# A bidirectional GLA and RWKV-7 encoder block: one-pass gate product, low-rank operands fetched a unit ahead, two operands made at another place

## The chip, the cores and the metric

The kernel is one program on one core of a Trainium2 chip. The metric is the device time in microseconds (us) of one execution, from start to end. A core has five engines with queues of their own: TensorE (PE), VectorE (DVE), ScalarE (ACT), GpSimd (POOL) and SyncE (SP); in this kernel SP issues all the DMAs.

## The reference

One layer on x of 2048 x 1024, all in float32:

```python
h = rmsnorm(x); p = h @ W_in                   # GLA | RWKV-7 | merge-gate columns
# GLA, 4 heads, forward (f) and backward (b): the decay of each step is a low-rank gate
la_f = log_sigmoid(af @ wa2_f + ba_f) / 16     # af: 16 columns of p; wa2: 16 x 256
la_b = log_sigmoid(ab @ wa2_b + ba_b) / 16
yA = (rmsnorm(gla(q, k, v, la_f) + flip(gla(flip(q, k, v, la_b)))) * silu(og)) @ proj
# RWKV-7, 8 heads, both directions
s = p + mu_prev * (shift_prev(p) - p) + mu_next * (shift_next(p) - p)
r, k, v, wl, al, gl = split(s)
w_dir = exp(-exp(-softplus(-(w0_dir + tanh(wl) @ w2_dir)) - 0.5))
a = sigmoid(a0 + al @ a2); g = sigmoid(gl) @ g2
kk = normalise(k * k_k); k = k * (1 + (a - 1) * k_a)
S = S * w + (S @ -kk)(kk * a)^T + v k^T; y = S r          # scan over 2048 steps
bonus = sum(r * k * r_k) * v
yB = ((groupnorm(y_f + y_b) + bonus) * g) @ proj
x = x + (sigmoid(gA) * yA + sigmoid(gB) * yB) @ W_out
x = rmsnorm(x + conv_glu(rmsnorm(x)))
```

## The kernel before

Products that need full precision are made of two float32r parts each: `split` rounds an operand to a high part and subtracts it for a low part, and `mm3` multiplies high by high, high by low and low by high. A float32 product without such parts is issued as two instructions.

The stages follow each other. First the norm of x and the v columns. Then `waf`, the 32 columns of the gates' low-rank input: for each of the 4 time blocks of 512 steps, 16 matmuls give 64 rows in PSUM (rows 0 to 31 from the weight's high part, 32 to 63 from its low part), which one copy puts into an `ev` buffer (a pool of three) and one store writes to the scratch `d_af` (L393 to L406). `gla_load` (L469) fetches a block of `d_af` for each of 4 heads x 4 blocks; `gla_gate` (L486) multiplies it by `wa2`, in which both row halves hold the same weights, in float32: `z` (L491).

The projections run tile by tile (`in_tile`, L373). Between their time blocks `Weave` steps a side generator: all of GLA first, then the RWKV preparation. The preparation goes over 4 head pairs p and 4 blocks b, which gives 16 units of `rwkv_prep(p, b)` (L725). A unit loads `twal`, the block of tanh(wl) and al (one buffer), and for b = 0 `lora`, the pair's weights; makes the shifted `sk`, `sr`, `sv`; multiplies `lora` by `twal` three times (L741 twice, L747 once, the tile `pw` has two banks); makes the scan's operands `arbk` (three buffers, L782 to L789), stored to `d_lt`; transposes v (L799, stored at L803); and makes the bonus (L805 to L812), for which `sr` is overwritten at L805 and multiplied by a matrix of ones at L807.

The order in each engine's queue, SP's DMA queue included, is chosen when the program is built, by a planning pass that goes by the order in the code and by modelled durations. Only the scan's main loop (L1283 on) keeps a hand-made order. The scan's start loads `Lt` tiles and makes scores (`sc_mm`, `sc_ev`), and between its pieces `fil(n)` takes n steps of the generator `fill` (L1127): the rest of the gate projections, four matmuls of 512 columns to a step (L1218). `w_get` loads a weight into the one `wraw` buffer (L1154), `w_put` splits it into `whi` and `wlo` (two buffers). The first step of the generator only loads the first weight; the second splits it and multiplies.

Of the kernel before, what the change touches and what calls it, by code (L numbers as in the profile page):

```python
# [104 lines left out]
def _pack(inputs):  # L105
# [8 lines left out]
    a["waf"] = kt(w[:, 1536:1568])  # L114
    wa = np.zeros((64, 4, 128), np.float32)
    f, b = one("gla_wa2_f"), one("gla_wa2_b")
    for h in range(4):
        for r0 in (0, 32):
            wa[r0:r0 + 16, h, :64] = f[:, h * 64:h * 64 + 64]
            wa[r0 + 16:r0 + 32, h, 64:] = b[:, h * 64:h * 64 + 64]  # L120
# [46 lines left out]
def _body(tc, A, out, dump=None, upto=99):  # L167
# [11 lines left out]

    def scratch(name, shape):  # L180
        return dr.tile(shape, F32, name=name, tag=name)

    d_gla = scratch("d_gla", [8, 128, T])
    d_vg = scratch("d_vg", [T, 512])
    d_af = scratch("d_af", [64, T])
    d_rw = scratch("d_rw", [14, 128, T])
# [212 lines left out]
    for b in range(NB):  # L399
        ps = pg.tile([128, 512], F32, name="pg", tag="pg")  # L400
        for i, xx in enumerate((hhi, hlo)):
            for k in range(KT):
                nc.tensor.matmul(ps[0:64, :], whi[:, k, 0:64], xx[b][:, k, :], start=(i == 0 and k == 0), stop=(i == 1 and k == KT - 1))
        o = ev.tile([128, 512], F32, name="ev", tag="ev")
        nc.scalar.copy(out=o[0:64, :], in_=ps[0:64, :])
        sync.dma_start(out=d_af[:, b * BT:(b + 1) * BT], in_=o[0:64, :])  # L406

# [15 lines left out]
    nc.vector.tensor_copy(out=gdiag, in_=gdf)  # L423
    wa2 = gp.tile([64, 4, 128], F32, name="wa2")
    sync.dma_start(out=wa2, in_=A["wa2"])
    dec = gp.tile([128, 4, 16], F32, name="dec")
# [42 lines left out]
    def gla_load(hs, b):  # L469
# [4 lines left out]
        ts = slice(b * BT, (b + 1) * BT)  # L474
        af = gp.tile([64, 512], F32, name="af", tag="af", bufs=1)
        sync.dma_start(out=af, in_=d_af[:, ts])
        q2 = gp.tile([128, 512], F32, name="q2", tag="q2", bufs=2)
# [245 lines left out]
    PE_ = {(d, j): nc.vector if (d, j) in DV else nc.gpsimd for d in range(2) for j in range(4)}  # L723

    def rwkv_prep(p, b):  # L725
        ts = slice(b * BT, (b + 1) * BT)
        cs = slice(b * 8, b * 8 + 8)
        pc = slice(p * 128, p * 128 + 128)
        twal = R["rp"].tile([128, 512], F32, name="twal", tag="twal")
        sync.dma_start(out=twal, in_=d_twal[:, ts])  # L730
        sk = shifted(3 + 3 * p, b, "sk")
        sr = shifted(2 + 3 * p, b, "sr")
        sv = shifted(4 + 3 * p, b, "sv")
        if b == 0:
            R["lora"] = R["rp"].tile([128, 2, 128], F32, name="lora", tag="lora")
            sync.dma_start(out=R["lora"], in_=A["lora"][:, :, pc])
        sg = []
# [15 lines left out]
        act_tail[0] = last  # L753
        yield

        tmp = R["rp"].tile([128, 512], F32, name="tmp", tag="tmp")
# [37 lines left out]
        yield  # L794
        nc.scalar.copy(out=tmp, in_=sv[:, ::-1])
        for d, sx in enumerate((sv, tmp)):
            pv = R["rs"].tile([128, 4, 128], F32, name="pv", tag="pv")
# [6 lines left out]
        yield  # L804
        nc.vector.scalar_tensor_tensor(out=sr, in0=sr, scalar=vc("rk", p), in1=kp, op0=ALU.mult, op1=ALU.mult)  # L805
        pn = R["rs"].tile([128, 512], F32, name="pn", tag="pn", bufs=2)
# [320 lines left out]
    def fill():  # L1127
# [39 lines left out]
        for i, u in enumerate(fresh):  # L1167
            if i:
                at(puts[i - 1], w_get, u)
            at(puts[i], w_put, u)  # L1170

# [31 lines left out]

        w_get(0)
        yield
        for i, (u, h, ph) in enumerate(order_):
# [26 lines left out]
    def fil(n=1):  # L1233
        for _ in range(n):
            next(fl, None)

    load_x(0)
    for e in range(2):
# [596 lines left out]
```

## Time and profile before

| | |
|---|---|
| three runs | 3526.49, 3528.93 (median), 3532.44 us |
| profiled execution: own time | 3531.8 us |
| its span, first to last instruction | 3530.0 us |
| mean granted clock of TensorE | 0.961 |
| instructions | 58016 |

The rows of the profile that are quoted below come from this one execution. Times in them are us from the start of the span unless marked ns. A line number is a line of the kernel before. The granted clock is a share of full speed; it has two levels, 1.2 and 2.4 GHz. Names of tiles stand without their numbers, so `wa` is `wa2`, and `whi` any of its buffers; `out<-in` is what an instruction writes and reads. A matmul's record includes its latency, so records in a row overlap; the distance from start to start is what one takes of the engine.

### The profile page before, as it was taken

Reading aid. Unit: us, or ns where it says so; the run is one execution under the profiler, and the core shown is the slowest. Engines: PE = TensorE matmul, PEld = TensorE weight load, DVE = VectorE, ACT = ScalarE, POOL = GpSimd, SP = SyncE. Lnnn points to the kernel's source line nnn. Section 1 sums busy time; section 2 is a strip of 40 time slices with the busy share of each in tenths; the row PEclk is TensorE's granted clock in tenths of the full one; section 3 lists DMA queues with packets and bytes.
Section 4 is the critical chain, followed back from the end, with each engine's and each line's share of the span. In section 5 each row is a group of like instructions: output and inputs, shape, how many; then the busy total and the mean of one; then the engine's idle time right before and its main releaser. Section 6 shows DMA issues by size and latency. Waiting matters only on the chain.

```text
span 3530.0 us, 58016 instructions
## 1 busy us (share of the span) xinstructions
PE 3282.4 (93%) x22232; PEld 2626.9 (74%) x22232; DVE 2281.4 (65%) x3903; ACT 1609.0 (46%) x2912; POOL 875.7 (25%) x715
## 2 busy tenths in 40 slices
PE   7999999999988888887777999999999999999999
PEld 6787778766656777766666788888877888878887
DVE  5207664587865666666776566888989989623222
ACT  4214443455545776776644333544454444411111
POOL 1122222134440000000002411666665555000000
PEclk9999999999999998998888999999999999999999
DMA  4233343687875455556788846422242222523222
GB/s 150 94 117 108 127 141 122 187 227 224 232 214 180 150 183 157 171 184 195 229 254 282 294 142 191 134 81 89 79 136 96 84 84 78 182 82 112 80 85 63
DMA packets 403222, 531.29 MB, mean 151 GB/s; under 512 B 61504, under 2 KB 250560, under 8 KB 402944
## 3 DMA queue, kind: packets, MB, share of 16 engines
q1 hardware_dynamic: 402944, 527.58, 48.0%
q8 instruction: 175, 2.87, 0.3%
q14 instruction: 103, 0.84, 0.1%
HBM read 345.02 MB, written 181.93 MB: 149 GB/s over the span
## 4 chain that ended last, share of the span: by engine, by line
PE 48%; DVE 12%; DMA 6%; ACT 4%; issue 2%; SPq 1%; POOL 0%; DVEq 0%; ACTq 0%; POOLq 0%
PE pu L1638 20%; PE pg L241 6%; PE pd L1722 4%; PE pd L1724 4%; PE pd L1723 4%; PE pf L1218 3%; DVE tm L924 1%; DVE XX L925 1%; DMA d_m<-ev 1%; DMA wraw<-win 1%; DVE X L1027 1%; DVE gX L1004 1%; DVE wlo L227 1%; ACT TT L938 1%; DMA ev<-d_gate 1%
## 5 line engine op out<-in xcount | busy, mean ns | idle before, releaser
L227 POOL TENSOR_TENSOR wlo<-wraw,whi 128x1024 fp32r<-128x1024 f32 x46 | 115.3, 2507 | 1175.0 <-ACT whi L226 929.1
L1561 POOL TENSOR_TENSOR rw<-rw 128x512 f32<-128x512 f32 x168 | 282.1, 1694 | 72.4 <-DVE s3l L227 59.7
L1722 PE MATMUL pd<-wdh,whi 128*128 128x512 f32 x672 | 261.6, 391 | 0.9 <-DVE ug L1506 0.9
L1723 PE MATMUL pd<-wdl,whi 128*128 128x512 f32 x672 | 261.4, 389 | 0.0
L1724 PE MATMUL pd<-wdh,wlo 128*128 128x512 f32 x672 | 259.3, 389 | 0.0
L1218 PE MATMUL pf<-fop,whi 128*128 128x512 f32 x576 | 178.6, 448 | 85.3 <-ACT whi L226 58.3
L241 PE MATMUL pg<-hlo,whi 128*128 128x512 f32 x928 | 254.2, 407 | 0.0
L241 PE MATMUL pg<-hhi,whi 128*128 128x512 f32 x928 | 249.7, 404 | 3.1 <-ACT whi L226 3.1
L241 PE MATMUL pg<-hhi,wlo 128*128 128x512 f32 x928 | 248.2, 402 | 0.0
L241 PEld LDWEIGHTS pg<-hhi,whi 128*128 128x128 f32 x928 | 176.2, 192 | 55.9 <-issue 15.8
L241 PEld LDWEIGHTS pg<-hlo,whi 128*128 128x128 f32 x928 | 176.9, 194 | 53.9 <-issue 18.1
L241 PEld LDWEIGHTS pg<-hhi,wlo 128*128 128x128 f32 x928 | 176.1, 192 | 50.6 <-issue 14.3
L1218 PEld LDWEIGHTS pf<-fop,whi 128*128 128x128 f32 x576 | 114.1, 209 | 122.1 <-ACT whi L226 64.1
L226 ACT CAST whi<-wraw 128x1024 fp32r<-128x1024 f32 x114 | 119.5, 1048 | 112.9 <-PE pg L241 54.1
L1606 DVE SCALAR_TENSOR_TENSOR cv<-ug,vec,cv 128x511 f32<-128x511 f32 (+1 forms) x88 | 124.1, 1410 | 57.4 <-ACT cv L1605 57.4
L1711 ACT CAST whi<-wraw 128x1024 fp32r<-128x1024 f32 (+1 forms) x36 | 35.3, 980 | 267.1 <-PE pd L1723 186.6
L1722 PEld LDWEIGHTS pd<-wdh,whi 128*128 128x128 f32 x672 | 126.1, 188 | 29.9 <-issue 4.2
L1724 PEld LDWEIGHTS pd<-wdh,wlo 128*128 128x128 f32 x672 | 126.1, 188 | 26.2
L1723 PEld LDWEIGHTS pd<-wdl,whi 128*128 128x128 f32 x672 | 126.1, 188 | 25.7
L1613 ACT ACTIVATE cv<-cv 128x511 f32<-128x511 f32 (+1 forms) x84 | 53.3, 634 | 197.0 <-DVE cv L1607 197.0
L1714 DVE TENSOR_TENSOR wlo<-wraw,whi 128x1024 fp32r<-128x1024 f32 (+1 forms) x36 | 39.3, 1091 | 151.4 <-ACT whi L1711 151.4
L227 DVE TENSOR_TENSOR wlo<-wraw,whi 128x1024 fp32r<-128x1024 f32 x68 | 84.1, 1237 | 79.3 <-ACT whi L226 79.2
(482 smaller groups left out, 8119.9 us busy)
## 6 DMA issues: line engine op xcount, KB each, us to landing
rw<-wup SPq DMA_DIRECT2D x84, 512.0 KB, 3.5
wraw<-win SPq DMA_DIRECT2D x74, 512.0 KB, 4.3
Lt<-d_lt SPq DMA_DIRECT2D x64, 512.0 KB, 5.2
d_lt<-arbk SPq DMA_DIRECT2D x96, 256.0 KB, 3.9
d_gate<-ev SPq DMA_DIRECT2D x64, 256.0 KB, 3.7
X<-d_vt SPq DMA_DIRECT2D x64, 256.0 KB, 4.4
bj<-d_lt SPq DMA_DIRECT2D x128, 128.0 KB, 3.8
d_m<-ev SPq DMA_DIRECT2D x64, 256.0 KB, 5.3
```

Of the source, the lines that this page charges most:

```text
L226: (hi_eng or nc.scalar.copy)(out=hi, in_=src)
L227: (lo_eng or nc.vector).tensor_tensor(out=lo, in0=src, in1=hi.bitcast(F32), op=ALU.subtract)
L241: nc.tensor.matmul(ps, (wh, wh, wl)[ph], (xh, xl, xh)[ph], start=(ph == 0 and i == 0), stop=(ph == 2 and i == n - 1))
L1218: nc.tensor.matmul(ps, (wh, wh, wl)[ph][:, k0 + k, :], (hi, lo, hi)[ph][:, k, :], start=i == first[u] and k == 0, stop=i == last[u] and k ...
L1561: ps_ = lambda o, x, y, op: nc.gpsimd.tensor_tensor(out=o, in0=x, in1=y, op=op)
L1606: nc.vector.scalar_tensor_tensor(out=c, in0=u[:, c0 - 1:c0 - 1 + n], scalar=vc("cw0", m), in1=c, op0=ALU.mult, op1=ALU.add)
L1613: nc.scalar.activation(out=g, in_=g, func=AF.Silu)
L1638: nc.tensor.matmul(ps, w_, x_, start=first and n == 0, stop=n == len(mm) - 1, skip_group_check=True)
L1714: nc.vector.tensor_tensor(out=al[:, 0:m], in0=raw[:, 0:m], in1=ah[:, 0:m].bitcast(F32), op=ALU.subtract)
L1722: nc.tensor.matmul(ps, a, wdh[k][:, cs], start=(k == 0), stop=False)
L1723: nc.tensor.matmul(ps, a, wdl[k][:, cs], start=False, stop=False)
L1724: nc.tensor.matmul(ps, l, wdh[k][:, cs], start=False, stop=False)
```

## The change

It has four parts. The gates' operand gets 128 rows: the high part of the first 32 rows of PSUM, its low part, the rows of the weight's low part, and the high part once more, against `wa2` in high part (96 rows) and low part (32 rows); the product is then one float32r instruction of 128 rows. For this each block makes a second `ev` tile with a subtraction and four stores rather than one. `twal` and `lora` are loaded by `get_low`, for the next unit, behind the present unit's third product in the code. The overwriting of `sr` stands ahead of the transposes of v. And `fil(1)` takes the first step of `fill` ahead of the scan's loads, with the first split in it; the later steps come one call sooner.

```diff
--- before.py
+++ after.py
@@ -112,10 +112,10 @@
     a["win"] = np.stack([kt(w[:, c]).reshape(128, 1024) for c in _in_tiles()])
     a["wv"] = kt(w[:, 512:1024])
     a["waf"] = kt(w[:, 1536:1568])
-    wa = np.zeros((64, 4, 128), np.float32)
+    wa = np.zeros((128, 4, 128), np.float32)
     f, b = one("gla_wa2_f"), one("gla_wa2_b")
     for h in range(4):
-        for r0 in (0, 32):
+        for r0 in (0, 32, 64, 96):
             wa[r0:r0 + 16, h, :64] = f[:, h * 64:h * 64 + 64]
             wa[r0 + 16:r0 + 32, h, 64:] = b[:, h * 64:h * 64 + 64]
     a["wa2"] = wa
@@ -177,12 +177,12 @@
 
     dr = pool(base, "dr", space=DRAM)
 
-    def scratch(name, shape):
-        return dr.tile(shape, F32, name=name, tag=name)
+    def scratch(name, shape, dt=F32):
+        return dr.tile(shape, dt, name=name, tag=name)
 
     d_gla = scratch("d_gla", [8, 128, T])
     d_vg = scratch("d_vg", [T, 512])
-    d_af = scratch("d_af", [64, T])
+    d_af = scratch("d_af", [128, T])
     d_rw = scratch("d_rw", [14, 128, T])
     d_gate = scratch("d_gate", [16, 128, T])
     d_oa = scratch("d_oa", [4, 128, T])
@@ -401,9 +401,13 @@
         for i, xx in enumerate((hhi, hlo)):
             for k in range(KT):
                 nc.tensor.matmul(ps[0:64, :], whi[:, k, 0:64], xx[b][:, k, :], start=(i == 0 and k == 0), stop=(i == 1 and k == KT - 1))
-        o = ev.tile([128, 512], F32, name="ev", tag="ev")
+
+        o = ev.tile([128, 512], F32R, name="ev", tag="ev")
+        ol = ev.tile([128, 512], F32R, name="ev", tag="ev")
         nc.scalar.copy(out=o[0:64, :], in_=ps[0:64, :])
-        sync.dma_start(out=d_af[:, b * BT:(b + 1) * BT], in_=o[0:64, :])
+        nc.vector.tensor_tensor(out=ol[0:32, :], in0=ps[0:32, :], in1=o[0:32, :].bitcast(F32), op=ALU.subtract)
+        for r0, src in ((0, o[0:32]), (32, ol[0:32]), (64, o[32:64]), (96, o[0:32])):
+            sync.dma_start(out=d_af[r0:r0 + 32, b * BT:(b + 1) * BT], in_=src.bitcast(F32))
 
 
     s1 = ExitStack()
@@ -421,8 +425,11 @@
     gdf = ev.tile([128, 512], F32, name="ev", tag="ev")[:, 0:128]
     sync.dma_start(out=gdf, in_=A["c_gdiag"])
     nc.vector.tensor_copy(out=gdiag, in_=gdf)
-    wa2 = gp.tile([64, 4, 128], F32, name="wa2")
-    sync.dma_start(out=wa2, in_=A["wa2"])
+    wa2 = gp.tile([128, 4, 128], F32R, name="wa2")
+    war = ev.tile([128, 4, 128], F32, name="ev", tag="ev")
+    sync.dma_start(out=war, in_=A["wa2"])
+    nc.scalar.copy(out=wa2, in_=war)
+    nc.vector.tensor_tensor(out=wa2[96:128], in0=war[96:128], in1=wa2[96:128].bitcast(F32), op=ALU.subtract)
     dec = gp.tile([128, 4, 16], F32, name="dec")
     b4 = [128, 4, 128]
     v4 = lambda t: t.rearrange("p (a b) -> p a b", a=4)
@@ -472,8 +479,8 @@
         qsrc = d_gla[(h // 2) * 2, r0:r0 + 64, :]
         ksrc = d_gla[(h // 2) * 2 + 1, r0:r0 + 64, :]
         ts = slice(b * BT, (b + 1) * BT)
-        af = gp.tile([64, 512], F32, name="af", tag="af", bufs=1)
-        sync.dma_start(out=af, in_=d_af[:, ts])
+        af = gp.tile([128, 512], F32R, name="af", tag="af", bufs=1)
+        sync.dma_start(out=af.bitcast(F32), in_=d_af[:, ts])
         q2 = gp.tile([128, 512], F32, name="q2", tag="q2", bufs=2)
         k2 = gp.tile([128, 512], F32, name="k2", tag="k2", bufs=2)
         for r in (0, 64):
@@ -722,18 +729,23 @@
 
     PE_ = {(d, j): nc.vector if (d, j) in DV else nc.gpsimd for d in range(2) for j in range(4)}
 
+    def get_low(p, b):
+        R["twal"] = R["rp"].tile([128, 512], F32, name="twal", tag="twal")
+        sync.dma_start(out=R["twal"], in_=d_twal[:, b * BT:(b + 1) * BT])
+        if b == 0:
+            R["lora"] = R["rp"].tile([128, 2, 128], F32, name="lora", tag="lora")
+            sync.dma_start(out=R["lora"], in_=A["lora"][:, :, p * 128:p * 128 + 128])
+
     def rwkv_prep(p, b):
         ts = slice(b * BT, (b + 1) * BT)
         cs = slice(b * 8, b * 8 + 8)
         pc = slice(p * 128, p * 128 + 128)
-        twal = R["rp"].tile([128, 512], F32, name="twal", tag="twal")
-        sync.dma_start(out=twal, in_=d_twal[:, ts])
+        if (p, b) == (0, 0):
+            get_low(0, 0)
+        twal = R["twal"]
         sk = shifted(3 + 3 * p, b, "sk")
         sr = shifted(2 + 3 * p, b, "sr")
         sv = shifted(4 + 3 * p, b, "sv")
-        if b == 0:
-            R["lora"] = R["rp"].tile([128, 2, 128], F32, name="lora", tag="lora")
-            sync.dma_start(out=R["lora"], in_=A["lora"][:, :, pc])
         sg = []
         last = act_tail[0]
         for d in range(2):
@@ -752,6 +764,8 @@
             last = nc.scalar.preload_act_table_set(LNEXP)
         act_tail[0] = last
         yield
+        if (p, b) != (3, NB - 1):
+            get_low(p + (b + 1) // NB, (b + 1) % NB)
 
         tmp = R["rp"].tile([128, 512], F32, name="tmp", tag="tmp")
         kk = R["rp"].tile([128, 512], F32, name="kkt", tag="kkt")
@@ -793,6 +807,7 @@
         act_tail[0] = fin
         yield
         nc.scalar.copy(out=tmp, in_=sv[:, ::-1])
+        nc.vector.scalar_tensor_tensor(out=sr, in0=sr, scalar=vc("rk", p), in1=kp, op0=ALU.mult, op1=ALU.mult)
         for d, sx in enumerate((sv, tmp)):
             pv = R["rs"].tile([128, 4, 128], F32, name="pv", tag="pv")
             for c in range(4):
@@ -802,7 +817,6 @@
             vs = slice((NB - 1 - b) * BT, (NB - b) * BT) if d else ts
             sync.dma_start(out=d_vt[vs, d, pc].rearrange("(c q) e -> q c e", q=128), in_=o.rearrange("p (a b) -> p a b", a=4))
         yield
-        nc.vector.scalar_tensor_tensor(out=sr, in0=sr, scalar=vc("rk", p), in1=kp, op0=ALU.mult, op1=ALU.mult)
         pn = R["rs"].tile([128, 512], F32, name="pn", tag="pn", bufs=2)
         nc.tensor.matmul(pn, bones, sr, start=True, stop=True)
         o = R["rp"].tile([128, 512], F32, name="pev", tag="pev", bufs=2)
@@ -1167,7 +1181,7 @@
         for i, u in enumerate(fresh):
             if i:
                 at(puts[i - 1], w_get, u)
-            at(puts[i], w_put, u)
+                at(puts[i], w_put, u)
 
         def o_new(k, b, h):
             ops[k, b, h] = [hb.tile([128, 4, BT], F32R, name="fop", **FOP) for _ in range(2)]
@@ -1202,6 +1216,7 @@
                 at(last[u], g_sig, u)
 
         w_get(0)
+        w_put(0)
         yield
         for i, (u, h, ph) in enumerate(order_):
             for f, a_ in sorted(todo.get(i, []), key=lambda x: x[0] not in (o_put, w_put)):
@@ -1234,6 +1249,7 @@
         for _ in range(n):
             next(fl, None)
 
+    fil(1)
     load_x(0)
     for e in range(2):
         for d in range(2):
```

## Rows read from the trace of the kernel before

**Rows 1.** The page, busy us, share and instructions of each engine.
```profile
PE 3282.4 (93%) x22232; PEld 2626.9 (74%) x22232; DVE 2281.4 (65%) x3903; ACT 1609.0 (46%) x2912; POOL 875.7 (25%) x715
```

**Rows 2.** Busy time by stage; columns as in the first line.
```profile
core 0: us, PE busy (x) PEld busy (x) DVE busy (x) ACT busy (x) POOL busy (x), PEclk, DMA share, GB/s
278.00:532.00 254.00, 252.41 (x1325) 195.16 (x1325) 186.19 (x445) 116.31 (x269) 62.36 (x49) 0.99 0.40 126
...
708.00:1047.00 339.00, 309.02 (x1147) 213.72 (x1146) 277.73 (x353) 190.80 (x287) 150.83 (x107) 0.92 0.80 223
1047.00:1110.00 63.00, 43.59 (x395) 33.87 (x394) 19.56 (x28) 29.53 (x69) 4.90 (x8) 0.84 0.77 238
```

**Rows 3.** Tile z: count, ns min/median/max, first and last start, forms.
```profile
L491 PE MATMUL z<-af,wa x32: 589/641/693, 278.1 to 527.7; 64*128 64x512 f32 x32
```

**Rows 4.** Timeline of PE around a gate product: start, us, instruction, count.
```profile
278.10 1.12 PE L491 MATMUL z<-af,wa 64*128 64x512 f32 x2
279.15 1.19 PE L241 MATMUL pg<-hhi,whi 128*128 128x512 f32 x4
280.18 2.00 PE L241 MATMUL pg<-hlo,whi 128*128 128x512 f32 x8
282.02 1.98 PE L241 MATMUL pg<-hhi,wlo 128*128 128x512 f32 x8
```

**Rows 5.** Waits of PE, 640 to 1050: us in total, times, longest.
```profile
PE pw L741 <- DMA twal<-d_twal: 17.6, 8, 3.2
PE pn L807 <- DVE sr L805: 5.0, 6, 1.2
PE pg L241 <- ACT whi L226: 3.1, 1, 3.1
```

**Rows 6.** Timeline of PE, low-rank products of three units, idle time before in brackets.
```profile
713.61 3.44 PE L741 MATMUL pw<-twal,lora 64*128 64x512 f32 x4 [2.66 <-DMA twal<-d_twal]
...
894.96 1.98 PE L741 MATMUL pw<-twal,lora 64*128 64x512 f32 x4
...
903.90 1.12 PE L747 MATMUL pw<-twal,lora 64*128 64x512 f32 x2
...
918.33 3.35 PE L741 MATMUL pw<-twal,lora 64*128 64x512 f32 x4 [1.89 <-DMA twal<-d_twal]
```

**Rows 7.** Busy time in two neighbouring units of the preparation, columns as before.
```profile
841.70:867.20 25.50, 25.50 (x107) 18.81 (x106) 18.14 (x25) 15.49 (x24) 9.38 (x8) 1.00 0.88 244
867.20:888.00 20.80, 16.81 (x54) 10.64 (x53) 16.24 (x23) 10.80 (x17) 9.30 (x8) 0.84 0.79 219
```

**Rows 8.** Waits of DVE, 700 to 1045.
```profile
DVE arbk L788 <- DMA d_lt<-arbk: 24.0, 13, 3.0
...
DVE kkt L765 <- ACT tmp L764: 10.5, 4, 5.0
DVE pev L809 <- PE pn L807: 4.8, 2, 3.6
```

**Rows 9.** Timeline of ACT, second of the four d_af blocks.
```profile
133.96 0.58 ACT L405 COPY ev<-pg 64x512 f32<-64x512 f32 x1 [3.10 <-PE pg L403]
```

**Rows 10.** Tile d_af: issue time of its stores, and time to landing.
```profile
L406 SPq DMA_DIRECT2D d_af<-ev x4: 445/449/470, 130.9 to 141.9; - x4
...
DMA to landing us min/median/max: 2.2/3.1/5.8
```

**Rows 11.** Timeline of SP's queue in one unit.
```profile
900.39 0.61 SPq L792 DMA_DIRECT2D d_lt<-arbk  x1
...
913.51 0.58 SPq L730 DMA_DIRECT2D twal<-d_twal  x1
```

**Rows 12.** Waits of SP's queue, 700 to 1045.
```profile
SPq L803 <- ACT pev L801: 12.5, 6, 6.4
```

**Rows 13.** Timeline of DVE, the bonus operand of one unit.
```profile
878.62 1.80 DVE L805 SCALAR_TENSOR_TENSOR sr<-sr,vec,kp 128x512 f32<-128x512 f32 x1 [2.21 <-POOL arbk L783]
```

**Rows 14.** Timeline of PE, the fill's first product.
```profile
1057.93 2.07 PE L1218 MATMUL pf<-hhi,whi 128*128 128x512 f32 x4 [8.84 <-ACT whi L226]
```

**Rows 15.** Timeline of SP's queue, the fill's first weight.
```profile
1052.54 0.59 SPq L1154 DMA_DIRECT2D wraw<-win  x1
```

## The prediction

> **What bounds the kernel now.** I read the page's first part, then the busy time of each engine by stage, then who waits for whom in the stages that the diff touches, and last the timelines of single places.
>
> Over the whole span TensorE (PE) is busy 93%, VectorE (DVE) 65% [rows 1]. A mean over 3530 us says little of a stage, so I cut out the three stretches in which the edits' work lies [rows 2]. From 278 to 532 us the gated-linear-attention (GLA) pieces run between projection matmuls: PE is busy 252.4 of 254 us at a granted clock of 0.99. That stretch is as long as PE's work. From 708 to 1047 (RWKV preparation between gate projections) PE is busy 309.0 of 339 with a mean clock of 0.92, DVE 277.7. From 1047 to 1110 the scan starts and PE is busy 43.6 of 63.
>
> In the RWKV stretch PE's idle time has few causes: 17.6 us for the low-rank tile twal, 5.0 us for the bonus operand sr, 3.1 for a weight [rows 5]. The twal waits cost more than their length. After the waits at 713.6 and 918.3 us the same four matmuls take 3.44 and 3.35 us, against 1.98 at 895.0 with no wait [rows 6]: the clock has fallen from 2.4 to 1.2 GHz. The mean clock of 0.92 over 339 us is 0.08 x 339 = 27 us of lost full-clock time [rows 2].
>
> But PE is not alone there. Take two neighbouring units of the preparation: 841.7 to 867.2 has no twal wait and PE is busy all 25.5 us; 867.2 to 888.0 has one, PE is busy 16.8 at clock 0.84 and still the unit is the shorter, since it holds fewer matmuls [rows 7]. So some units are PE's, and in others DVE, SyncE's queue (SP) and the stores hold the pace. DVE's own list says this: it waits 24.0 us for stores to free its arbk tiles, and only 10.5 (kkt, through ScalarE from a matmul) and 4.8 (pev) for what PE makes [rows 8].
>
> **The change, part by part.**
>
> *Gate product.* It removes 16 fp32 products (32 instructions) of 64 rows and puts in 16 of one pass. One starts at 278.10 and the next matmul at 279.15: 1.05 us; eight one-pass matmuls of 512 columns then take 280.18 to 282.02, 0.23 each [rows 4]. The 641 ns a record [rows 3] is latency, and overlaps; the starts are what counts. 16 x (1.05 - 0.23) = 13.1 us, in a stretch where PE is the limit and hardly waits. DVE at 186.2 of 254 has room. All that follows starts that much sooner. Bounds: 0 if DVE or SP took it all, 13.1 at most; I take 13.1. The Trainium skill (FP8 and Floating Point Precision, TensorE Precision Notes) counts four passes for true fp32; by that figure the removed product is 4 x 0.23 = 0.92 us, the saving 16 x 0.69 = 11.0, and the sum 2 us poorer; the row has 1.05, and decides.
>
> *Making the 128-row operand.* Four times: one DVE subtraction of 32 rows by 512 columns (nearest row: ScalarE's copy of 64 such rows, 0.58 us [rows 9]), a second ev buffer, and four stores for one. Before, ScalarE empties such a product in 0.58 us and waits 3.10 for the next: one each 3.68 [rows 9]. A pair of ev buffers is held for 0.58 + 0.58 + 4 x 0.45 (SP's time for a store) + 3.1 to land [rows 10] = 6.1 us; with three buffers a pair is had each 4.0 us. The fourth is late by 4 x 0.3 = 1.3 us, and the three PSUM banks that PE fills in 11 us cover that. I take 0; without that cover up to +4. The setup's extra split (one copy, one subtraction) falls while PE multiplies: 0. The af load is twice as large. The 16 gates lie some 17 us apart (278.1 to 527.7 [rows 3]), and even the slowest d_af transfer lands in 5.8 [rows 10]: 0.
>
> *Low-rank operands ahead.* twal and lora are now asked for a unit before their use. Before, SP issues twal at 913.51 [rows 11] and PE wants it at 918.33 - 1.89 = 916.4 [rows 6]. The 17.6 us of PE waits go, and with them most of the 27 us of half clock. What is late next is DVE. Upper bound: all of PE's idle time and the clock, 30 + 27 = 57 us. Lower bound: 0, if DVE and SP don't care. DVE can move up only by what it loses to PE: 10.5 + 4.8 = 15.3 us [rows 8]; its busy 277.7 and its other waits of some 46 stay. I take 15.3, since both ends are far and this row is the limit nearest to PE's. It could reach 25: SP stands 12.5 us for d_vt's source tiles [rows 12], which come from matmuls, and the arbk stores queue behind them; with those sooner some 10 of DVE's 24.0 may go too. The load overwrites the tile, so it waits for the unit's third product, and behind it in SP's queue stand the d_lt stores; see the rivals.
>
> *Bonus operand.* The product overwrites sr, and in DVE's queue it already stands right behind sr's last reader: L805 starts at 878.62, after 2.21 us of waiting for POOL's L783, which reads sr [rows 13]. It can't go earlier: 0. Bounds: -5.0 (PE's wait for it [rows 5]) to +2.2 (that wait once more, where it is queued sooner).
>
> *First fill weight.* PE waits 8.84 us for it until 1057.93 [rows 14]. SP issues its load at 1052.54, at once behind the preparation's last d_lt stores and as the first of the scan's loads [rows 15]. Asking sooner in the text doesn't move it past those stores. The second weight comes one step sooner: I take -1 us. Bounds: -8.8 to +3 (a step's shift in the scan's hand-made order).
>
> Sum against the profiled execution: 3531.8 - 13.1 - 15.3 - 1 = 3502.4. The median of the runs is 2.9 below that execution, so 3500 by the runs' measure. A difference of 0.2% (7 us) is about what a measurement can tell from none.
>
> **The rivals.**
>
> *DVE and SP hold the RWKV stretch.* PE's saved waits come back as waits for DVE's sr, which is there already [rows 5], and for sv and hs. For it: the shorter of the two units is the one in which PE waits [rows 7]. Against it: PE fills others to the brim. Then only the gate counts: 3531.8 - 13.1 - 2.9 = 3516. The Trainium skill (Perfetto Trace Analysis, Identifying the Most-Contended Engine) would have TensorE judged by weight-load time, which is 63% here against DVE's 82%, and DVE optimised first; by that rule relief of PE brings nothing in this stretch, and the time is this rival's.
>
> *The prefetch blocks SP.* The twal load must wait for L747, which runs at 903.9, 8.9 us after L741 at 895.0 [rows 6]. If it sits in SP's queue ahead of the d_lt stores that SP issues from 900.39 on [rows 11], these come late, DVE waits longer for arbk tiles (13 times now [rows 8]), and PE for DVE. A block of 3 us a unit is 16 x 3 = 48 us: 3529 - 13 + 48 - 15 = 3549. From 28/16 = 1.8 us a unit on, all gain is gone. For it: SP is in order and already waits for other engines [rows 12]. Against: the queue order is made from modelled times, and the load would be put where the product is expected to be done.
>
> *It doesn't do what it says.* The order is remade by the program's own planning, and new waits in the GLA stretch and a changed start of the scan eat the gate's saving: 3529.
>
> **How the numbers follow.** Forecast (both gains, 3484 to 3512) 0.60; DVE and SP hold 0.17; nothing 0.09; SP blocked 0.14. So faster 0.77, same 0.09, slower 0.14. Low end: 13.1 + 25 + 7 = 45 below, 3484, with 0.05 left below it. The high end takes in "nothing", 3531, and leaves the blocked queue out: 0.19 in all. The forecast's own range is 3484 to 3512.
>
> **What the profile after would show.** Gate: 16 records of z on 128 rows, the next matmul 0.23 us behind; the RWKV stretch some 13 us sooner. Prefetch: no PE wait on twal, mean clock from 0.92 to 0.97 or more, DVE's waits for tmp and pn near zero, the stretch some 15 us shorter, with PE waiting for sr, sv or hs in its place. Fill: the 8 us wait still there. The prediction is wrong if SP's waits at twal's line are microseconds long, if DVE's wait for arbk stores grows past 24 us, or if PE stands during the four d_af products.

## The result: slower, and where the profile after has the time

The changed kernel takes 3545.89 us in the median (3543.74 to 3547.26) where the kernel before, run beside it, takes 3528.53 (3524.17 to 3532.44): a ratio of 1.0052, 95% interval 1.004 to 1.0064, slower by 17 us or 0.5%. The forecast was 3500 and faster, the range 3484 to 3531.

The step that was surest came out. Tile z after, to be held against [rows 3]:

```profile
L498 PEld LDWEIGHTS z<-af,wa x16: 187/188/192, 277.9 to 515.0; 128*128 128x128 f32 x16
L498 PE MATMUL z<-af,wa x16: 388/393/476, 278.1 to 515.2; 128*128 128x512 f32 x16
```

Sixteen products where there were 32 instructions, and the last one starts at 515.2 instead of 527.7, 12.5 us sooner over the same sixteen gates. Four stores in place of one did not stop PE.

The step with the largest term did not. PE's waits in the RWKV units after, to be held against [rows 5]:

```profile
PE pw L753 <- DMA twal<-d_twal: 16.6, 8, 4.5
PE pn L821 <- DVE sr L810: 8.7, 7, 4.0
PE pv L814 <- ACT tmp L809: 7.5, 1, 7.5
PE pw L753 <- DMA lora<-lora: 5.2, 2, 2.9
```

The load that is written a unit ahead still makes PE wait 16.6 us, eight times. The queue of SP and the timeline of PE in one unit say why:

```profile
853.94 0.61 SPq L826 DMA_DIRECT2D d_bon<-pev  x1
854.64 0.54 SPq L389 DMA_DIRECT2D d_gate<-ev  x1
855.23 0.46 SPq L826 DMA_DIRECT2D d_bon<-pev  x1
855.78 1.43 SPq L734 DMA_DIRECT2D twal<-d_twal  x1
```

```profile
848.57 1.12 PE L759 MATMUL pw<-twal,lora 64*128 64x512 f32 x2
862.58 3.78 PE L753 MATMUL pw<-twal,lora 64*128 64x512 f32 x4 [4.45 <-DMA twal<-d_twal]
```

There is one twal tile. Its last reader, L759, starts at 848.57, and the next unit's first reader wants it at 862.58 - 4.45 = 858.1. So "a unit ahead" is at most 9 us ahead, and in SP's queue the load stands behind the unit's stores, as it did before [rows 11]. The four products behind the wait again take 3.78 us where the same four took 1.98 without one [rows 6].

Where then did 17 us come from? The span cut into the same stages in both, before and then after (length, busy time of PE, PEld, DVE, ACT and POOL, PE's clock, DMA share, GB/s):

```profile
278.10:637.80 359.70, 356.58 (x1876) 282.67 (x1875) 236.20 (x593) 151.99 (x362) 86.45 (x70) 1.00 0.40 128
637.80:1047.70 409.90, 379.92 (x1437) 267.10 (x1438) 315.56 (x404) 225.78 (x344) 162.70 (x115) 0.94 0.77 218
1047.70:1166.50 118.80, 95.67 (x1155) 76.84 (x1153) 58.58 (x113) 67.01 (x147) 4.90 (x8) 0.89 0.57 176
1166.50:1867.40 700.90, 575.14 (x9541) 472.51 (x9533) 483.51 (x964) 462.62 (x996) 0.00 (x0) 0.90 0.64 192
1867.40:3037.10 1169.70, 1132.89 (x4978) 929.62 (x4976) 953.82 (x1208) 529.83 (x766) 571.76 (x485) 0.98 0.41 136
```

```profile
278.10:625.00 346.90, 344.00 (x1882) 284.91 (x1880) 238.10 (x593) 153.41 (x365) 86.44 (x70) 1.00 0.46 140
625.00:1041.00 416.00, 375.61 (x1427) 263.33 (x1428) 316.21 (x406) 229.65 (x349) 165.32 (x119) 0.93 0.79 217
1041.00:1155.00 114.00, 93.43 (x1146) 74.69 (x1145) 58.80 (x112) 62.87 (x138) 1.12 (x4) 0.87 0.55 169
1155.00:1879.30 724.30, 577.52 (x9559) 473.38 (x9551) 487.22 (x970) 464.70 (x1000) 0.00 (x0) 0.89 0.64 187
1879.30:3049.20 1169.90, 1129.17 (x4957) 925.85 (x4955) 947.97 (x1202) 529.64 (x764) 571.27 (x485) 0.98 0.42 136
```

The stages are: GLA up to the first RWKV product; the RWKV units; the scan's start; the scan itself, from the first to the last store of its rows; the merge, output products and most of the feed-forward. GLA is 12.8 us shorter. Units and start together are 528.7 before and 530.0 after. The scan is 23.4 us longer (700.9 to 724.3), more than the whole loss. Behind it the two are equal (1169.7 and 1169.9), but that is two effects that cancel, as e13_after_pad shows below. The profiled executions differ by 12 us in span, the medians by 17. No term of the prediction had the scan's length in it, but for +3 us as a bound of the fill weight.

### The profile page after: what moved, and what is told of

It reads as the page before. It is cut to its first block, busy times and chain, and to the rows that moved or that the text cites. A ratio compares the mean times of both kernels' runs of the same rounds, so it can differ in the third digit from the quotient of the medians.

```text
span 3542.0 us, 58030 instructions
## 1 busy us (share of the span) xinstructions
PE 3263.2 (92%) x22216; PEld 2621.4 (74%) x22216; DVE 2285.7 (65%) x3908; ACT 1613.1 (46%) x2913; POOL 874.0 (25%) x715
## 4 chain that ended last, share of the span: by engine, by line
PE 53%; DVE 11%; DMA 9%; ACT 4%; issue 3%; POOL 1%; SPq 1%; DVEq 0%; ACTq 0%; POOLq 0%
PE pu L1654 21%; PE pg L241 8%; PE pd L1738 4%; PE pd L1739 4%; PE pd L1740 4%; PE pf L1233 4%; DMA d_m<-ev 1%; DMA wraw<-win 1%; DVE tm L938 1%; DMA d_lt<-arbk 1%; DVE XX L939 1%; ACT whi L226 1%; PE psc L888 1%; DVE X L1041 1%; DVE gX L1018 1%
```

## The experiments

Times are medians; ratios are to the kernel before, run beside it on the same chip. "Units" is from the first to the last store of the bonus (d_bon), "scan" from the first to the last store of its rows (d_y), both in the profiled execution.

**The parts alone.** First each part by itself, and the change without its fill part.

The gate part alone: the hunks for wa2, d_af and af of the diff.

> The gate product alone; nothing else of the change. Theory A (the loss comes with the fill's shift by one step, in the scan): the RWKV preparation starts about 13 us sooner, the scan from its first to its last state store takes 701 us as before, and the time is 7 to 13 us below the kernel before, 3516 to 3522. Rival B (any remade order of SP's queue lengthens the scan): the scan takes 715 us or more and the time is 3528 or above. Rival C (the RWKV stretch gives the gate's saving back): it ends less than 5 us sooner than before.

3536.76 us, ratio 1.0022 (1.001 to 1.0034); units 347.8, scan 709.2.

The loads alone: get_low and its two calls.

> The earlier request for the low-rank operands alone. Theory A: twal is still issued behind the bonus stores, PE waits some 17 us for it as before, the time is within 6 us of the kernel before (3523 to 3535). Rival B: the scan takes 715 us or more. Rival C: the RWKV stretch grows by 5 us or more, by new waits for lora and for DVE's and ScalarE's products.

3538.69 us, 1.0028 (1.0018 to 1.0039); units 346.3, scan 705.8.

The fill part alone: the first weight made ahead of the first piece, and `fil(1)` ahead of `load_x(0)`.

> The first fill weight made sooner alone, with the step's shift that comes with it. Theory A: all up to the scan is as before, the scan takes some 20 us longer than before (720 us from first to last state store against 701), the time is 3540 to 3550. Rival B: the scan is as before and the time 3526 to 3531.

3542.68 us, 1.0039 (1.0025 to 1.0053); units 336.0, scan 723.1.

All but the fill part: gate, loads and bonus operand.

> The change without its fill part: gate product, low-rank operands and bonus operand. Theory A: the scan takes about 701 us and the time is 3514 to 3524, some 7 to 13 us below the kernel before. Rival B (the remade order of the queues is the cause): the scan takes 715 us or more, the time is 3535 or above.

3539.03 us, 1.0026 (1.0015 to 1.0037); units 345.4, scan 722.5.

Every part alone costs, the gate part with its 12.8 us saved too. The fill part lengthens the scan by 22 us, but so does the rest without it, so the theory that the fill shift is the whole loss falls. Gate and loads alone came out 15 and 4 us above what their first theories allowed. The loads fit their rival C: from the first RWKV product to the first store of the scan's rows they take 537.9 us, where before takes 528.7. They do shorten the wait that they were meant for, which I had expected to stay at 17 us, but PE then waits for DVE's sr instead. PE's waits in the units of e2_low, against 17.6 and 5.0 before [rows 5]:

```profile
PE pn L814 <- DVE sr L812: 10.6, 6, 4.1
PE pw L746 <- DMA twal<-d_twal: 9.7, 6, 2.7
```

In gate, loads and nofill TensorE, ScalarE and VectorE keep before's order in the scan; only some transfers in SP's queue stand elsewhere. The hand-made order of the scan's loop is that of the four computing engines; SP's transfers in it are planned like all others.

**Do stages repeat?** The kernel before again, with the low-rank weights' load one place sooner in its unit:

```
         sync.dma_start(out=twal, in_=d_twal[:, ts])
+        if b == 0: ... sync.dma_start(out=R["lora"], in_=A["lora"][:, :, pc])
         sk = shifted(3 + 3 * p, b, "sk")
```

> The kernel before, with one load (the low-rank weights, four times in the whole kernel) moved up behind the other low-rank load in its unit: every engine's order in the RWKV units and in the scan stays what it was. Its use is the length of the stages in another execution. If an execution repeats its stages (the scan took 700.9 us from the first to the last store of its rows in the one traced so far, the RWKV units 339.6), they come out within 3 us of that, and the 22 us by which the scan grew are the kernels'. If stages scatter from execution to execution, the scan comes out anywhere from 695 to 725, and the stage times of single traces carry little.

One execution, 3535.76 us: units 338.6 and scan 702.7, against 339.6 and 700.9. In this pair the stages repeat within 2 us. The kernels below that keep before's order in the scan have 700.1 to 706.5 (e12_soon, e17_dram256k, e9_dram, e18_dram1m), the last of them without any loss of time. So a scan of 723 belongs to the kernel; one of 709 is only 3 us beyond that one.

**A prefetch with somewhere to go.** The loads part with the operand in the ring of three eviction tiles and two weight buffers; then the same with the gate part.

```
-        R["twal"] = R["rp"].tile([128, 512], F32, name="twal", tag="twal")
+        R["twal"] = ev.tile([128, 512], F32, name="ev", tag="ev")
-            R["lora"] = ... tag="lora")
+            R["lora"] = ... tag="lora", bufs=2)
```

> The low-rank loads of the change alone, but with somewhere to go: the operand takes one of the three eviction tiles, which nothing uses in this stage, and the weights get two buffers. Theory: the loads of the change stayed behind the last products that read the one tile, so nothing was fetched ahead; with a free tile the waits of the first products for this operand (17.6 us before, 16.6 after the change) go, and the RWKV units shorten by 10 to 17 us against the loads alone (346.3), the kernel by as much: 3522 to 3529. Rival: those waits stand in for the vector engine's work, as I took it for a part of them in the prediction: they go to other rows, the units stay within 5 us of 346, and the time at 3533 to 3541. A third: the planner's new order lengthens the scan anyway (over 715), and the time is above 3541.

> The gate product in one pass and the low-rank loads with a free tile and two weight buffers, without the other two parts. Theory: 12.8 us less in the gate product, 10 to 17 less in the RWKV units than the gate alone had there (347.8), so the first faster kernel of this family: 3510 to 3525. Rival: the waits go to other rows and the saving of the gate is given back as in the gate alone: 3530 to 3540.

3575.48 us, 1.0137 (1.0118 to 1.0156), and 3577.84 us, 1.0137 (1.0119 to 1.0154): both far outside what I expected. The wait itself went, as PE's waits in the units of e6_low_ev show:

```profile
PE pn L814 <- DVE sr L812: 18.2, 9, 5.5
PE pw L746 <- ACT sig L749: 6.1, 2, 3.7
...
PE pw L746 <- DMA ev<-d_twal: 2.1, 1, 2.1
```

From 17.6 us to 2.1, and in its place PE waits 18.2 for DVE's sr, where it waited 5.0 [rows 5]. As in e2_low, that is the prediction's first rival. My premise was wrong as well: the projections of this stage evict through that ring. With it shared, the planner starts the RWKV units sooner, ahead of projection products that used to cover the end of GLA. PE's timeline there:

```profile
608.74 4.21 PE L711 MATMUL pn<-gh,g 128*128 128x512 f32 x9 [15.56 <-ACT gh L226]
612.97 1.98 PE L746 MATMUL pw<-ev,lora 64*128 64x512 f32 x4
```

The first RWKV product runs at 612.97 instead of 637.8 and the first store of the scan's rows comes at 1208.7 instead of 1166.5. This run shows what replaces the wait, but it does not price a prefetch in a free buffer of its own; that stays untried.

**The start of the scan.** The change without its fill part, with the block from `load_x(0)` to `st_g(0)` moved behind the first four pieces of preparation, which puts ScalarE's first copy of the scan back near its old place.

> The change without its fill part (scan of 722.5 us in one trace, 3539 in all), with the request for the first rows of the scan moved in the source behind the first four pieces of its preparation, which puts the first copy of the scan on ScalarE back to within 13 instructions of where the kernel before has it, instead of 89. If the scan's length is set by that start, it comes out at 700 to 709 and the kernel at 3518 to 3530; if it is not (the scatter of executions, or the few transfers in another order), at 715 to 725 and 3536 to 3542.

3542.06 us, 1.0038 (1.0023 to 1.0054), scan 717.1: the start does not set the length. Where the scan grows does. Time from the first store of the scan's rows to that of step 4, 12, ... in each kernel (starts of the d_y stores in SP's queue):

| kernel | step 4 | 12 | 22 | 26 | 28 | 31 |
|---|---|---|---|---|---|---|
| before | 83.2 | 257.7 | 478.2 | 570.0 | 634.1 | 700.9 |
| e5_control | 84.0 | 256.4 | 477.3 | 570.6 | 635.0 | 702.6 |
| e2_low | 82.1 | 255.6 | 475.4 | 570.7 | 634.2 | 705.8 |
| e1_gate | 82.8 | 255.2 | 477.0 | 575.4 | 640.7 | 709.1 |
| e4_nofill | 83.7 | 257.8 | 478.3 | 575.0 | 643.9 | 722.5 |
| e3_fill | 86.1 | 266.5 | 494.1 | 589.1 | 648.4 | 723.0 |
| after | 87.2 | 265.7 | 494.4 | 587.6 | 647.1 | 724.2 |

The growths differ: with the fill part 16 us by step 22 and 8 to 10 more behind step 28; in e1_gate and e4_nofill 5 to 7 us between 22 and 26 (in the whole change 1.4); and in e4_nofill 12 us behind step 28. The first two then got pairs of their own.

**The place of the scratch in DRAM.** With d_af twice as large, every scratch tensor declared behind it starts 512 KB later. (That is taken from the declarations; the traces hold no addresses.) e9_dram is the kernel before with nothing but this move. e10_gate_pad is the gate part with the move undone: d_af is declared last, and an unused tensor of the old size, with one store of 64 KB into it, keeps its old place. But for that store all engines keep the order of the kernel that each is held against.

```
-    d_af = scratch("d_af", [64, T])          # e9: 128 rows, only the first 64 used
+    d_af = scratch("d_af", [128, T])
```

```
-    d_af = scratch("d_af", [128, T])         # e10, on the gate part
+    d_pad = scratch("d_pad", [64, T])
...
     d_mat = scratch("d_mat", [8, 128, 4, BT])
+    d_af = scratch("d_af", [128, T])
```

> The kernel before, whose low-rank gate scratch in DRAM is declared with 128 rows of which 64 are used, so that the scratch tensors declared behind it start 512 KB later, as they do in the change; every instruction and its order stay. Theory: in the four kernels with the gate part the stores of the gate projections land later in the scan (3.5 or 3.6 us in the median against 2.4 to 3.1 in those without it), and so do the loads of them (3.8 to 4.3 against 3.2 to 3.4 in steps 22 to 26), which is the new place of the scratch: here those rows too come out at 3.5 and 3.9 or more, steps 22 to 26 of the scan take 96 to 98 us where before they took 92 and 93, and the kernel 3534 to 3542. Rival: the place does nothing, landing times and stages stay within 3 us of before's, and the kernel at 3525 to 3532.

> The gate part alone, with its scratch of 128 rows declared last and one of 64 rows left where it was (one store of 64 KB goes there), so that all other scratch tensors lie where they lay before; all engines' orders are those of the gate part alone, which took 3536.8. Theory: the stores and loads of the gate projections land as before, and the scan (709.2), the out products and the feed-forward stage (2 to 3 us longer each with the gate part) come back: 3524 to 3531; the RWKV units stay at 344 to 348, because their planned order is not touched. Rival: the place does nothing: 3534 to 3540.

e9_dram: 3542.34 us, 1.003 (1.0017 to 1.0044). e10_gate_pad: 3517.88 us, 0.9957 (0.9945 to 0.997). The move alone makes the kernel before 13 us slower by the medians, 11 by the ratio. Undoing it makes the gate part some 20 us faster than it was and faster than the kernel before, and 6 us better than the 3524 to 3531 that I expected. The transfers say the same. From step 22 of the scan on, 100 us, SP's transfers with their KB and the median us from issue to landing, in before, in e9_dram and in e10_gate_pad:

```profile
d_m<-ev SPq DMA_DIRECT2D x11, 256.0 KB, 3.4
ev<-d_gate SPq DMA_DIRECT2D x11, 256.0 KB, 3.3
wraw<-wpa SPq DMA_DIRECT2D x5, 512.0 KB, 5.7
...
ev<-d_oa SPq DMA_DIRECT2D x5, 256.0 KB, 4.4
```

```profile
d_m<-ev SPq DMA_DIRECT2D x11, 256.0 KB, 4.3
ev<-d_gate SPq DMA_DIRECT2D x10, 256.0 KB, 3.9
wraw<-wpa SPq DMA_DIRECT2D x5, 512.0 KB, 8.0
...
ev<-d_oa SPq DMA_DIRECT2D x5, 256.0 KB, 5.6
```

```profile
wraw<-wpa SPq DMA_DIRECT2D x6, 512.0 KB, 6.1
d_m<-ev SPq DMA_DIRECT2D x11, 256.0 KB, 3.9
ev<-d_gate SPq DMA_DIRECT2D x10, 256.0 KB, 3.2
...
ev<-d_oa SPq DMA_DIRECT2D x5, 256.0 KB, 4.5
```

These four land later at the moved place (the output weights wpa, which are no scratch, among them) and at the old one near where they landed before, d_m in between; e12_soon, with before's places, has 3.6, 3.5, 6.3 and 4.8 for them in the same stretch. Not all transfers are slower: Q<-d_g lands at 7.2 before, 6.5 in e9_dram and 6.3 in e10_gate_pad. The scan takes 705.7 against 700.9 us in e9_dram and 703.5 against 709.2 in e10_gate_pad, and the stretch behind it says more: from the scan's last store to the first down product e9_dram takes 1177.1 us where before takes 1169.7, and e10_gate_pad 1168.0 where e1_gate takes 1178.2. e9_dram's stores of the gate projections, over steps 0 to 22, land at 3.0 and not at the 3.5 that I expected; that row did not tell the two apart.

**The two halves of the fill part.**

```
+    fil(1)                    # e11_shift: this alone
     load_x(0)
```

```
         w_get(0)
+        w_put(0)              # e12_soon: the weight sooner ...
         yield
+        yield                 # ... and an empty piece, so that nothing shifts
                              # (with fil(1) and the moved line at puts[i] of the diff)
```

> Of the fill part only the extra first piece, so that each product of the background work in the scan comes one piece earlier; its first weight is still made where it was. Theory: the shift is what lengthens the scan (16 of its 22 us lay between steps 4 and 24, where the products have another order): scan 715 to 725, time 3537 to 3545. Rival: it is the weight made sooner: scan 698 to 706, time 3524 to 3532.

> Of the fill part only the first weight made sooner; an empty piece keeps every product of the background work at its old place in the scan, whose orders are those of before. Theory: the shift is what costs: scan 698 to 706 and time 3523 to 3531. Rival: the weight made sooner costs: scan over 712, time over 3535.

e11_shift: 3543.83 us, 1.0035 (1.0023 to 1.0048), scan 724.3. e12_soon: 3528.12 us, 0.9997 (0.9987 to 1.0007), scan 700.1. The weight made sooner is worth nothing (PE still waits 16.3 us in three places for the fill's weights ahead of the scan), and the shift of the background products by one piece is the whole cost of this part. In the scan from about step 2 to step 12 the same 3408 matmuls take 219.0 us in e12_soon and 226.5 in e11_shift. TensorE's order around the scan's own product pw, at the same place of the scan in the one and in the other:

```profile
1255.09 1.15 PE L990 MATMUL pw<-X,Lt 128*64 128x64 f32 x32
...
1259.03 1.21 PE L1220 MATMUL pf<-hhi,whi 128*128 128x512 f32 x4 [1.86 <-ACT whi L226]
```

```profile
1264.43 1.28 PE L1218 MATMUL pf<-hhi,whi 128*128 128x512 f32 x4 [4.17 <-ACT whi L226]
1265.63 1.98 PE L990 MATMUL pw<-X,Lt 128*64 128x64 f32 x32
```

In both kernels the last sixteen matmuls ahead of this pw are background products (pf), so the shift does not put more of them there. What changes is which: the piece that starts on a new weight, and waits for ScalarE to make it, stood behind pw and now stands ahead of it, so the scan's chain waits too. From step 1 to 22, PE's waits of over 0.3 us in background products with pw next behind them add up to 28.5 us in e12_soon and 42.8 in e11_shift: 14 us of the 16 by which e11_shift is behind at step 22 (493.3 against 476.9). From step 28 on it loses again (77.2 us against 66.4), and behind the scan it gains: from the last store of the rows to the first down product it takes 1156.0 us where e12_soon takes 1165.0. So 24 us in the scan make 12 to 15 in the time.

**Do the causes add up?** The whole change, and the change without its fill part, both with the scratch restored as in e10_gate_pad.

> The whole change, with its 128-row scratch declared last and one of 64 rows left in its old place, so that every other scratch tensor lies where it lay before. If place and shift are what made the change slower, this gives back 13 to 19 us of the change's 3546 and keeps the shift's 15: 3527 to 3533, no different from before. If the place matters only beside the gate part's own orders, it stays at 3538 to 3546.

> The whole change without its fill part (3539 with the scratch moved), the place of the scratch restored. By the sum of the causes 13 to 19 us less: 3520 to 3526. Its last steps of the scan keep the gate load that stands ahead of a load of the scan's rows in SyncE's queue, so steps 28 to 31 take 75 us or more where before they take 67; by that alone it stays behind the gate part with the place restored (3517.9). Rival: that swap costs nothing once the loads land sooner: steps 28 to 31 at 67 to 70 and the time at 3516 to 3520.

3528.96 us, 0.9994 (0.9985 to 1.0003), and 3521.03 us, 0.9973 (0.9963 to 0.9982): both inside what the causes give. The whole change, with nothing altered but where a tensor lies, is no slower than before. Its scan is as long as in the change (724.3): the place costs it nothing there. What comes back lies on both sides: 524.0 us where the change takes 530.0 from the first RWKV product to the first store of the scan's rows, and 1161.2 where it takes 1169.9 from the last such store to the first down product. In e14_nofill_pad the scan takes 709.0 us, 75.0 of it behind step 28 where before takes 66.8. SP's queue in step 29, before and then there:

```profile
1822.39 0.56 SPq L1048 DMA_DIRECT2D Q<-d_g  x1
1823.06 0.62 SPq L975 DMA_DIRECT2D X<-d_vt  x1
1823.78 0.54 SPq L1037 DMA_DIRECT2D d_y<-ys  x1
1824.61 0.45 SPq L975 DMA_DIRECT2D X<-d_vt  x1
1826.70 0.33 SPq L1194 DMA_DIRECT2D ev<-d_gate  x1
```

```profile
1807.69 0.55 SPq L1065 DMA_DIRECT2D Q<-d_g  x1
1812.33 0.33 SPq L1211 DMA_DIRECT2D ev<-d_gate  x1
1812.77 0.45 SPq L992 DMA_DIRECT2D X<-d_vt  x1
1813.31 0.54 SPq L1054 DMA_DIRECT2D d_y<-ys  x1
1813.90 0.45 SPq L992 DMA_DIRECT2D X<-d_vt  x1
```

The load of a gate, which needs a free eviction tile, is planned ahead of the load of the scan's next rows. It stands 4.1 us in the queue (SP's waits put 4.0 of it down to the store of d_m out of such a tile), and the rows stand behind it. By that store the kernel is 4 us behind before, counted from the scan's first store, and by the last 8 us. No run undoes this swap by itself. But of the twenty kernels the eight with a gate load just ahead of these rows take 73.8 to 79.9 us from step 28 on, and the other twelve 66.4 to 71.6. One of the eight is e15_replan below, which has before's work and before's scratch places, and e14_nofill_pad's order of transfers in the scan.

**The planned order of the units.** Two kernels with the pacing constant of the projections changed: the kernel before at 2.35, and e10_gate_pad at 2.2.

```
-RATE_A = 2.4
+RATE_A = 2.35        # e15_replan; 2.2 in e16_gate_pad_replan
```

> The kernel before with one pacing constant of its projections at 2.35 instead of 2.4: the same instructions, but the planner puts the RWKV units in another order (187 of TensorE's 272 instructions there stand as before). Theory: the order of before is a good one among many, and any other costs: the units take 343 to 348 us where before's order takes 335 to 340, and the kernel 3533 to 3540. Rival: the order makes no difference, and what lengthened the units in the gate part and in the loads part is those parts: the units at 335 to 340.

> The gate part with the place restored (3517.9, units 345.9) and the same pacing constant at 2.2, a planned order of the units closer to before's (257 of 272 on TensorE) and the scan's transfers almost in before's order. If the order is what costs, the units come out at 336 to 342 and the kernel at 3508 to 3515; if it is the gate part itself, at 344 to 348 and 3515 to 3521.

3534.13 us, 1.0011 (1.0002 to 1.0019), units 344.1; and 3516.5 us, 0.9964 (0.9951 to 0.9976), units 348.3. So another order alone does lengthen the units of the kernel before by 4.5 us with no work changed, but an order that stands nearer to before's did not shorten those of the gate part. And the question was partly put wrong, since the next stretch gives it back. From the first RWKV product to the first store of the scan's rows it is 528.7 us before, 529.8 in e15_replan, 527.0 in e10_gate_pad and 524.4 in e16_gate_pad_replan; the loads alone (537.9) are clearly longer, apart from the two kernels that share the eviction ring. What e15_replan loses, it loses in the scan (710.9), with 75.8 us behind step 28, as in e14_nofill_pad.

**Which places cost?** The kernel before with 96 and 192 rows declared for d_af, the scratch behind it 256 KB and 1 MB later.

> The kernel before with 96 rows declared for the gate scratch, so that all scratch behind it starts 256 KB later. If any move costs (before's place is a good one among many), 3533 to 3545. If the cost comes from the 512 KB offset in particular, no change: 3525 to 3532, with steps 22 to 26 of the scan at 91 to 94 us.

> The same with 192 rows, 1 MB later. If what matters repeats with the megabyte (most of these tensors are multiples of 1 MB long), the time is that of before: 3525 to 3532, steps 22 to 26 at 91 to 94 us. If any move costs, 3533 to 3545 and 96 to 98 us.

3535.78 us, 1.0022 (1.0011 to 1.0033), and 3525.49 us, 0.9983 (0.9973 to 0.9994). The cost is 8 us at 256 KB, 13 at 512 KB and gone at 1 MB, so not every move costs. The three fit a cost that goes by the offset within the megabyte, but one multiple of it is too few to show that, and at 1 MB the time is 3 us below before's, with an interval that leaves out 1. The stretch behind the scan, to the first down product, puts the four in the order of their times: 1167.2 us at 1 MB, 1169.7 before, 1171.3 at 256 KB, 1177.1 at 512 KB. The scan does not: 706.5, 700.9, 703.9 and 705.7. Steps 22 to 26 took 98.4 and 95.1 us; the second is above the 91 to 94 that I had put down.

## Why the prediction was wrong

The sum had five terms (-13.1, 0, -15.3, 0, -1) and none for what the edits do to the order and the place of other work. Three steps failed: the operand's 0, which left out the scratch that it moves (11 to 20 us); the operands ahead at -15.3, which brought nothing; and the first weight at -1 with +3 as its worst, whose shift costs 7 to 15. By the ratios, against the 3529 us of before, the runs build up the result like this: the gate part in before's scratch places is -15 us (0.9957), loads and bonus operand add 6 (0.9973), the fill part 7 (0.9994), and the moved scratch 20 (1.0052). Each of these carries some 5 us of uncertainty, and the second is hardly clear of nothing (by the medians it is 2).

- *Gate product, -13.1.* Right: 12.5 us on the row and 12.8 on the stretch. It reached the end only with the scratch restored. The Trainium skill (FP8 and Floating Point Precision, TensorE Precision Notes) counts four passes for true fp32, by which I had estimated 11.0 us for the removed products; the trace agrees in kind and has some 2 us more.
- *Making the 128-row operand, 0.* As work it was right, PE did not stand. What failed is that I counted its DMAs and not its memory: the 64 added rows move every scratch tensor declared behind, at a cost of 11 to 13 us on the kernel before and of some 20 with the gate part. The step was an edit costed at nothing, whose price falls in stages that it does not touch. No row of before shows it, but the diff line did.
- *Low-rank operands ahead, -15.3.* Wrong in its premise. The text did note that the load waits for the unit's third product, but then took the waits as gone. The margin could be read before: L747 at 903.90 and the next unit's products ready at 916.4 [rows 6] leave 12.5 us, in which SP's stores stand. Alone the part costs 10 us. Where the wait shrank (9.7 us in e2_low) or went (2.1 in e6_low_ev), PE's waits moved to sr, as the rival "DVE and SP hold the RWKV stretch" had it. The view behind [rows 12] had more for that rival than the line quoted from it: SP's longest waits there are for DVE, 23.8 us for arbk (L792) and 21.5 for sk (L690). The page that I set beside that rival, from the Trainium skill (Perfetto Trace Analysis, Identifying the Most-Contended Engine), would have put VectorE first in this stretch; e2_low and e6_low_ev agree as far as the 10.6 and 18.2 us on sr go. SP was not blocked either, and 3549 came near the measured time by other means.
- *Bonus operand, 0.* Not run alone. With the loads it makes the 2 to 6 us above; what is its share stays open.
- *First fill weight, -1.* The weight sooner is worth 0 (e12_soon), as argued. The bound of +3 for "a step's shift in the scan's hand-made order" was the failed size: the shift alone costs 12 to 15 us in the kernel before, and 7 to 8 within the change. I priced it as one lost step, but in the new order waits for new weights stand ahead of the scan's chain again and again: 14 us of them by step 22.
- *"It doesn't do what it says".* This rival named the remade order and a changed start of the scan. The order does cost (e15_replan, +4 us, with the swap in step 29), the start does not (e8_nofill_x), and the loss was larger than the gate's saving.

Of the three signs that I had named for a wrong prediction none came: no wait of SP at twal's line is among its eleven largest, which end at 3.4 us, DVE waits 17.6 us for arbk stores where it waited 24.0 [rows 8], and PE did not stand during the d_af products. All three lay in the stages up to the scan, and the loss lay for the most part in the scan and behind it.

Left open: why the place of the scratch matters, also to transfers of tensors that are no scratch, what the swap in step 29 costs by itself, and what a prefetch with its own buffer would bring. The fastest versions are e10_gate_pad and e16_gate_pad_replan, 3517.9 and 3516.5 us, both faster than the kernel before by 0.4%.

## What to carry to other kernels

An edit to a tuned kernel with a planned order is three edits: the work, the order that is planned anew, and the addresses of everything declared behind a tensor that grew; run the last two as placebos, with the work unchanged, before the work is blamed. A prefetch is only as far ahead as the last reader of the buffer that it fills: take that reader's time and the next use from the timeline before giving it a gain. A hand-made interleave is timed to the piece: a shift by one piece can put the piece that waits ahead of the chain, so it is priced over all its steps and not once.

## What the hardware showed that was not expected

Where the scratch tensors lie in DRAM is worth up to 13 us of 3529 with every instruction the same: +8 us at 256 KB, +13 at 512 KB, -3 at 1 MB. At 512 KB, 256 KB transfers of the moved tensors landed 0.6 to 1.2 us later in the median (3.3 to 3.9, 3.4 to 4.3, 4.4 to 5.6) and a 512 KB load of weights that are no scratch 2.3 us later (5.7 to 8.0), in a stretch where the DMA engines are busy about three quarters of the time. With before's places another execution (e12_soon) has 3.5, 3.6, 4.8 and 6.3 there, so a part of each difference is scatter.
